# A transformer block on one core: gate, embedding projection and final norm laid out by tokens, the residual turned by VectorE and placed by SBUF-to-SBUF DMA

## The chip, the cores and the metric

One core of one Trainium2 chip runs the whole block in one program. The metric is the device time of an execution in microseconds; three executions of the kernel before were timed. The trace is of one further execution, with a span (first to last instruction) and a time of its own.

## The reference, cut to what matters

512 tokens, width 1024, float32. A mixer (mLSTM heads and sparse attention) and its output projection come first, then a convolutional feed-forward, then a gated per-layer embedding and a final norm:

```python
x = x + jnp.concatenate([m_out, a_out], axis=-1) @ w_out[i]
x = x + conv_ffn(rms_norm(x, ln2_g[i]), w_up[i], conv_w[i], conv_b[i], w_down[i])   # d_ff 2048
gate = jax.nn.sigmoid(rms_norm(x, ple_norm_g[i]) @ w_ple_gate[i])                   # 1024 x 1024
x = x + gate * (p[i] @ w_ple_proj[i])                                               # p: 512 x 256
return rms_norm(x, final_g)
```

with `rms_norm(x, g) = x * rsqrt(mean(x * x) + 1e-6) * g` over the 1024 features of a token.

## The kernel before, in words

Activations lie by features: the residual `X` is [128 features, 8 blocks, 512 tokens], so a sum over features runs over partitions and blocks, and a factor that belongs to a token is a row along the free dimension that has to be spread over all partitions. Every product in full precision is three matmuls in float32r: each operand is split into a high part (ScalarE copy, names ending in h) and a low part (VectorE subtraction, ending in l), and high times high, high times low and low times high are summed in PSUM. Weight blocks of 512 KB come in by SP's DMA queue into two raw buffers, are split into two pairs of buffers, and are used in the order of a list of jobs (`st`). A scheduler decides how the instructions of the code are interleaved on each engine; each engine then runs its list in order, and waits where an operand is not ready.

The last part of the program, which the change touches:

- **Down jobs** `wd{b}{half}` (b = 0 to 7): 48 matmuls of 512 columns into `pd{b}`; VectorE adds to `X[:, b]`, `sum_squares` makes the gate's operands `x3h`, `x3l` from it and adds squares to `acc3`.
- **Norm n3** (`start_norm`): four small matmuls sum `acc3` over partitions, VectorE does a reciprocal square root by Newton steps on [128 tokens, 4] (`n3yc`), four PE transposes and a ScalarE copy spread it as rows (`n3rb`).
- **Gate, output blocks 0 to 3** (`g0` to `g3`, `pg`): 24 matmuls of 512 columns each; the weight block is the stationary operand, the tokens move. `ple_evac` then multiplies by `n3rb` (VectorE), takes tanh (ScalarE), combines with the projected embedding `pp` and adds to `X` (VectorE), squares (ScalarE) and adds the squares into `acc4` (VectorE), and scales by the final gain (ScalarE).
- **Gate, blocks 4 to 7**: the weights `wgr` are split into `wres` and stay; two parts of 256 tokens, in each 4 x 24 matmuls of 256 columns, so that the first 256 tokens can be finished early.
- **End** (`start_finish`, `finish`): for the first part the sums, Newton steps, two PE transposes (`n40pb`) and products on GpSimd and VectorE run beside the second part's matmuls. For the second part a matmul with ones sums and spreads in one (`n4ps`), then follow a ScalarE reciprocal square root, three VectorE steps on 128x256, and products and output DMAs by feature blocks.

The embedding's projection `pp_job` runs much earlier, between the mLSTM heads, with 48 matmuls of 512 columns.

## Time and profile before

| | us |
|---|---|
| three timed executions | 646.04, 646.11, 647.53 (median 646.11) |
| the profiled execution's own time | 645.6 |
| its span | 643.8 |
| PE busy in the span | 623.0 (97%) |
| VectorE (DVE) busy | 429.9 (67%) |
| ScalarE (ACT) busy | 318.8 (50%) |
| GpSimd (POOL) busy | 42.7 (7%) |

The span leaves out 1.8 us of the profiled time. A busy share is a mean over stages that have different limits, so the stages at the end are read one by one.

### The profile page before, as it was taken

Reading aid. Unit: us, or ns where it says so; the run is one execution under the profiler, and the core shown is the slowest. Engines: PE = TensorE matmul, PEld = TensorE weight load, DVE = VectorE, ACT = ScalarE, POOL = GpSimd, SP = SyncE. Lnnn points to the kernel's source line nnn. Section 1 sums busy time; section 2 is a strip of 40 time slices with the busy share of each in tenths; the row PEclk is TensorE's granted clock in tenths of the full one; section 3 lists DMA queues with packets and bytes.
Section 4 is the critical chain, followed back from the end, with each engine's and each line's share of the span. In section 5 each row is a group of like instructions: output and inputs, shape, how many; then the busy total and the mean of one; then the engine's idle time right before and its main releaser. Section 6 shows DMA issues by size and latency. Waiting matters only on the chain.

```text
span 643.8 us, 8563 instructions
## 1 busy us (share of the span) xinstructions
PE 623.0 (97%) x3099; PEld 505.1 (78%) x3099; DVE 429.9 (67%) x868; ACT 318.8 (50%) x663; POOL 42.7 (7%) x92
## 2 busy tenths in 40 slices
PE   8997999999999999999999999999999999999993
PEld 6886877777777777787788888888888888888892
DVE  6898558888878977784876565655555334346766
ACT  7457445677656755654645333333343323233642
POOL 0400005211111200000000000000000000000003
PEclk9999999999999999999999999999999999999997
DMA  8712044311121153012233222222332323233203
GB/s 327 282 30 87 2 130 108 89 34 38 62 67 33 36 195 98 34 48 83 67 113 100 94 94 94 97 96 98 99 98 99 99 98 99 98 99 115 82 1 131
DMA packets 19673, 60.39 MB, mean 94 GB/s; under 512 B 2280, under 2 KB 4712, under 8 KB 19564
## 3 DMA queue, kind: packets, MB, share of 16 engines
q1 hardware_dynamic: 18096, 57.43, 26.9%
q0 software_dynamic: 1248, 2.16, 1.5%
q8 instruction: 24, 0.39, 0.2%
q10 hardware_dynamic: 288, 0.28, 0.2%
q14 instruction: 17, 0.14, 0.1%
HBM read 56.18 MB, written 2.10 MB: 91 GB/s over the span
## 4 chain that ended last, share of the span: by engine, by line
PE 82%; DVE 10%; ACT 4%; issue 1%; DMA 1%; DVEq 0%; ACTq 0%
PE pu L415 8%; PE pu L419 8%; PE pu L416 8%; PE pd L415 5%; PE pd L416 5%; PE pd L419 5%; PE pt L784 2%; PE pmq L416 2%; PE pmq L415 2%; PE pmq L419 2%; PE pv L792 2%; PE pmv L332 1%; PE pg L407 1%; PE ms L953 1%; PE pc L368 1%
## 5 line engine op out<-in xcount | busy, mean ns | idle before, releaser
L1075 ACT ACTIVATE u<-zv 128x512 fp32r<-128x512 f32 x16 | 10.1, 633 | 45.3 <-DVE zv L1073 45.3
L1072 DVE TENSOR_TENSOR zv<-pu,n2rb 128x512 f32<-128x512 f32 x16 | 11.1, 691 | 31.3 <-PE pu L419 31.3
L787 ACT ACTIVATE ph<-pt 128x512 fp32r<-128x512 f32 x40 | 23.5, 597 | 17.0 <-PE pt L784 16.4
L757 POOL TENSOR_SCALAR E<-E,rr 128x512 f32<-128x512 f32 (+3 forms) x32 | 21.2, 663 | 159.7 <-DVE rr L754 113.4
L788 DVE TENSOR_TENSOR pl<-pt,ph 128x512 fp32r<-128x512 f32 x40 | 27.0, 684 | 6.6 <-ACT ph L787 6.2
L1062 DVE TENSOR_TENSOR zg<-pu,n2rb 128x512 f32<-128x512 f32 x16 | 11.1, 692 | 26.0 <-PE pu L419 24.6
L784 PE MATMUL pt<-cols,E 128*128 128x128 f32 x160 | 27.8, 275 | 0.4 <-DVE E L759 0.3
L1088 DVE TENSOR_TENSOR X<-pd,X 128x512 f32<-128x512 f32 x8 | 5.5, 691 | 31.9 <-PE pd L419 31.9
L784 PEld LDWEIGHTS pt<-cols,E 128*128 128x128 f32 x160 | 20.0, 140 | 7.2 <-DVE E L759 2.6
L1065 ACT ACTIVATE cv<-zg,cols 128x512 f32<-128x512 f32 x16 | 13.1, 816 | 20.1 <-DVE zg L1062 20.1
L1068 ACT ACTIVATE cv<-cv 128x512 f32<-128x512 f32 x16 | 10.1, 631 | 24.6 <-DVE cv L1067 24.6
L751 ACT ACTIVATE E<-s,nm 128x384 f32<-128x384 f32 (+2 forms) x48 | 22.2, 471 | 0.0
L265 DVE TENSOR_TENSOR acc<-acc,sq 128x512 f32<-128x512 f32 (+1 forms) x30 | 19.1, 636 | 0.9 <-ACT sq L261 0.7
L792 PE MATMUL pv<-ph,V 128*128 128x512 f32 x40 | 18.7, 467 | 0.4 <-ACT ph L787 0.3
L261 ACT ACTIVATE sq<-X 128x512 f32<-128x512 f32 (+1 forms) x24 | 13.5, 560 | 11.0 <-DVE X L1129 11.0
L407 PE MATMUL pg<-x3h,wres 128*128 128x256 f32 x64 | 18.3, 285 | 0.0
L1076 DVE TENSOR_TENSOR u<-zv,u 128x512 fp32r<-128x512 f32 x16 | 11.1, 692 | 10.5 <-ACT u L1075 10.5
L408 PE MATMUL pg<-x3l,wres 128*128 128x256 f32 x64 | 18.1, 283 | 0.0
L409 PE MATMUL pg<-x3h,wres 128*128 128x256 f32 x64 | 18.1, 283 | 0.0
L1061 POOL MEMSET zg<- 128x2 f32 x16 | 1.5, 99 | 243.3 <-DVE cv L1067 150.7
L794 PE MATMUL pv<-pl,V 128*128 128x512 f32 x40 | 16.7, 418 | 0.0
L741 DVE TENSOR_REDUCE nm<-s 128x2 f32<-128x768 f32 (+2 forms) x24 | 16.4, 682 | 0.0
(1052 smaller groups left out, 2024.3 us busy)
## 6 DMA issues: line engine op xcount, KB each, us to landing
X<-in_xg SPq DMA_DIRECT2D x1, 2048.0 KB, 8.3
wgr<-in_w_pg SPq DMA_DIRECT2D x4, 512.0 KB, 3.6
s1r<-in_w_s SPq DMA_DIRECT2D x3, 672.0 KB, 9.0
xT<-in_xg SPq DMA_DIRECT2D x3, 514.0 KB, 8.3
rawx<-in_cmp_w SPq DMA_DIRECT2D x3, 512.0 KB, 6.3
Q<-hlq POOLq DMA_DIRECT2D x12, 128.0 KB, 3.4
out_y<-X SPq DMA_DIRECT2D x5, 256.0 KB, 2.2
rawx<-in_w_in SPq DMA_DIRECT2D x2, 512.0 KB, 11.1
```

The costliest lines, as they stand in the source:

```text
L265: return VE.tensor_add(acc[:, :n], acc[:, :n], sq[:, :n])
L407: TE.matmul(ps, wh[:, kw], rh[:, kx, n], start=first, stop=False)
L408: TE.matmul(ps, wh[:, kw], rl[:, kx, n], start=False, stop=False)
L415: TE.matmul(ps, wh[:, w], rh[:, x, n], start=first and j == 0, stop=False)
L416: TE.matmul(ps, wh[:, w], rl[:, x, n], start=False, stop=False)
L419: TE.matmul(ps, wl[:, w], rh[:, x, n], start=False, stop=last and j == len(kx) - 1)
L751: SE.activation(e, p, AF.Exp, bias=nm[:, b:b + 1], accum_out=rs[:, b:b + 1])
L757: GE.tensor_scalar(e, e, rr[:, b:b + 1], 0.0, op0=ALU.mult, op1=ALU.add)
L784: TE.transpose(pt[:, r * 128:(r + 1) * 128], Es[r][:, c0:c0 + 128], ident)
L787: SE.activation(ph, pt, AF.Copy)
L788: VE.tensor_sub(pl, pt, f32(ph))
L792: TE.matmul(pv, vs, ph, start=first, stop=False)
```

## The change

Gate, embedding and final norm are computed with tokens on the partitions. The gate's stationary operand is now a block of 128 tokens of `x3h` or `x3l`, and 512 columns of weights move past it (`psg[t]` for the first half of the output features, `pg1{t}` for the second). The n3 factor of a token is then one number per partition and goes in as the scale of the tanh (`sc`); the rows `n3rb` and their transposes go. The sum of squares of a token is a sum along the free dimension, taken by the squaring instruction's accumulator into `ss`; the n4 factor is one number per partition too. The last 128 tokens' second half is computed in two pieces of 256 columns (`CUT`), and only that last tile uses the ScalarE reciprocal square root; the others use Newton steps on [128, 1]. GpSimd has no part in it any more. The final gain comes as a full tile `gF`.

The residual has to be turned for this: after each down job VectorE transposes `X[:, b]` in squares of 32 (`turn`), and after blocks 3 and 7 sixteen DMAs each, from SP's queue, move 32 partitions' worth from `xturn` to their place in `xo` (`moves`; 64 KB each, in runs of 512 bytes). The features of a token come out permuted; the weights' columns are permuted on the way in and the output on the way out, outside the timed program. `pp_job` computes the projection by tokens, with the operands in exchanged roles.

The diff, cut to the new code; the bodies of the functions of the same names that stand above go out.

```diff
     def pp_job(c):
         def run(wh, wl):
+            for t in range(NT):
+                ts = slice(t * 128, (t + 1) * 128)
+                ps = pG(f"ppp{c}{t}")
+                for k in range(2):
+                    TE.matmul(ps, phl[:, 0, k, ts], wh[:, k], start=k == 0, stop=False)
+                    TE.matmul(ps, phl[:, 1, k, ts], wh[:, k], start=False, stop=False)
+                    yield 0.43
+                for k in range(2):
+                    TE.matmul(ps, phl[:, 0, k, ts], wl[:, k], start=False, stop=k == 1)
+                    yield 0.22
+                SE.activation(ppt[NT * c + t], ps, AF.Copy, scale=0.5)
+        st.add(f"pp{c}", a["w_pp"][:, c], [128, 2, 512], run)
...
     def start_norm(norm, acc, name):
         def stats():
             yc = rstd_stats(acc, name)
+            if norm is n3:
+                norm["yc"] = yc
+                return
...
+    xturn = [None]
+
+    def turn(b, dst):
+        VE.transpose(dst[:, :, :, b % 4].rearrange("p t c j -> p (t c) j"),
+                     X[:, b].rearrange("p (c j) -> p c j", j=32))
+        if b % 4 == 3:
+            for q in range(4):
+                st.after(T_TURN * (1 + q), lambda q=q: moves(b // 4, q, dst))
+
+    def moves(g, q, src):
+        for c in range(4):
+            nc.sync.dma_start(xo[32 * c:32 * c + 32, :, q // 2, q % 2 * 256 + g * 128:q % 2 * 256 + g * 128 + 128],
+                              src[32 * q:32 * q + 32, :, c].rearrange("p t b j -> p t (b j)"))
...
     def down_job(b, half):
...
+                if b % 4 == 0:
+                    xturn[0] = fpool.tile([128, NT, 4, 4, 32], F32, bufs=1, name=f"xturn{b}", tag="xturn")
+                st.after(T_TURN, lambda: turn(b, xturn[0]))
...
+    xo = fpool.tile([128, NT, 2, 512], F32, bufs=1, name="xo")
...
+    gF = main.tile([128, 2, 512], F32, tag="mixa", name="gF")
+    nc.sync.dma_start(gF, a["gF"])
+    ss = fpool.tile([128, NT, 3], F32, bufs=1, name="ss")
+    sc = fpool.tile([128, NT], F32, bufs=1, name="sc")
+
+    def scale_of():
+        yc = n3["yc"]
+        VE.tensor_scalar(sc, yc, 0.5, None, op0=ALU.mult)
 
+    def ple_evac(t, h, ps, c0, c1, part):
+        z = t2k("zz")[:, c0:c1]
+        last = SE.activation(z, ps[:, c0:c1], AF.Tanh, scale=sc[:, t:t + 1])
+        VE.scalar_tensor_tensor(z, z, 1.0, ppt[NT * h + t][:, c0:c1], op0=ALU.add, op1=ALU.mult)
+        o = xo[:, t, h, c0:c1]
+        VE.tensor_add(o, o, z)
+        sq = t2k("sq")
+        if t == NT - 1 and part == 2:
             pre = SE.activation(warm, epsc, AF.Abs_reciprocal_sqrt)
             behind(pre, last, "the table is loaded behind the last tanh")
+            VE.scalar_tensor_tensor(sq[:, c0:c1], o, 1.0, o, op0=ALU.mult, op1=ALU.mult,
+                                    accum_out=ss[:, t, part:part + 1])
         else:
+            SE.activation(sq[:, c0:c1], o, AF.Square, accum_out=ss[:, t, part:part + 1])
+
+    def finish(t):
+        orow = out[t * 128:(t + 1) * 128].rearrange("p (h n) -> p h n", h=2)
+        v = small.tile([128, 1], F32, tag="nrv", name=f"n4v{t}")
+        if t < NT - 1:
+            VE.tensor_add(v, ss[:, t, 0:1], ss[:, t, 1:2])
+            VE.tensor_scalar(v, v, 1.0 / D, EPS, op0=ALU.mult, op1=ALU.add)
+            y = newton_rsqrt(v, 1, f"n4{t}")
+            SE.activation(xo[:, t, 0], xo[:, t, 0], AF.Copy, scale=y)
+            VE.scalar_tensor_tensor(xo[:, t, 1], xo[:, t, 1], y, gF[:, 1], op0=ALU.mult, op1=ALU.mult)
+            nc.sync.dma_start(orow, xo[:, t])
+            return
+        VE.scalar_tensor_tensor(v, ss[:, t, 2:3], 1.0 / D, vlast, op0=ALU.mult, op1=ALU.add)
+        y = small.tile([128, 1], F32, tag="nry", name="n4y")
+        w = small.tile([128, 1], F32, tag="nrt", name="n4w")
+        u = small.tile([128, 1], F32, tag="nru", name="n4u")
+        SE.activation(y, v, AF.Abs_reciprocal_sqrt)
+        VE.tensor_scalar(u, v, -0.5, None, op0=ALU.mult)
+        VE.tensor_mul(xo[:, t, 1, CUT:], xo[:, t, 1, CUT:], gF[:, 1, CUT:])
+        VE.scalar_tensor_tensor(w, y, u, y, op0=ALU.mult, op1=ALU.mult)
+        VE.scalar_tensor_tensor(w, w, 1.5, y, op0=ALU.add, op1=ALU.mult)
+        SE.activation(xo[:, t, 0], xo[:, t, 0], AF.Copy, scale=w)
+        VE.tensor_scalar(xo[:, t, 1], xo[:, t, 1], w, None, op0=ALU.mult)
+        nc.sync.dma_start(orow[:, 1], xo[:, t, 1])
+        nc.scalar.dma_start(orow[:, 0], xo[:, t, 0])
...
+    CUT = 512 - LASTW
+    vlast = fpool.tile([128, 1], F32, bufs=1, name="vlast")
+    sa = pSa("pga")
+    psg = [sa[:, 0], sa[:, 1], pG("pg2"), pG("pg3")]
+
+    def gate_job(c):
         def run(wh, wl):
+            for t in range(NT):
+                ts = slice(t * 128, (t + 1) * 128)
+                for j in range(2):
+                    k = 2 * c + j
+                    TE.matmul(psg[t], x3h[:, k, ts], wh[:, j], start=k == 0, stop=False)
+                    TE.matmul(psg[t], x3l[:, k, ts], wh[:, j], start=False, stop=False)
+                    TE.matmul(psg[t], x3h[:, k, ts], wl[:, j], start=False, stop=k == KB - 1)
+                    yield 0.66
+                if c == 3 and t < 3:
+                    ple_evac(t, 0, psg[t], 0, 512, 0)
+            if c == 2:
+                scale_of()
+        st.add(f"g{c}", a["w_pg"][:, 0, 2 * c:2 * c + 2], [128, 2, 512], run)
+
+    for c in range(4):
+        gate_job(c)
+    wres = [main.tile([128, KB, 512], F32R, tag="B16", bufs=3, name=f"wres{i}") for i in range(2)]
+    for c in range(4):
+        st.until(f"g{c}")
+        raw = wpool.tile([128, 2, 512], F32, tag="raw", bufs=2, name=f"wgr{c}")
+        nc.sync.dma_start(raw, a["w_pg"][:, 1, 2 * c:2 * c + 2])
+        SE.activation(wres[0][:, 2 * c:2 * c + 2], raw, AF.Copy)
+        VE.tensor_sub(wres[1][:, 2 * c:2 * c + 2], raw, f32(wres[0][:, 2 * c:2 * c + 2]))
+
+    for t in range(NT):
+        ts = slice(t * 128, (t + 1) * 128)
+        ps = (pSb, pV, pT, pT)[t](f"pg1{t}")
+        cuts = ((0, 512),) if t < NT - 1 else ((0, CUT), (CUT, 512))
+        for part, (c0, c1) in enumerate(cuts):
+            if part:
+                ps = pG("pg1last")
             for k in range(KB):
+                TE.matmul(ps[:, c0:c1], x3h[:, k, ts], wres[0][:, k, c0:c1], start=k == 0, stop=False)
+                TE.matmul(ps[:, c0:c1], x3l[:, k, ts], wres[0][:, k, c0:c1], start=False, stop=False)
+                TE.matmul(ps[:, c0:c1], x3h[:, k, ts], wres[1][:, k, c0:c1], start=False, stop=k == KB - 1)
+                if part == 0 and k == 1 and t == 0:
+                    ple_evac(3, 0, psg[3], 0, 512, 0)
+                if part == 0 and k == 5:
+                    VE.tensor_mul(xo[:, t, 0], xo[:, t, 0], gF[:, 0])
+            ple_evac(t, 1, ps, c0, c1, 1 + part)
+            if t == NT - 1 and part == 0:
+                VE.tensor_mul(xo[:, t, 1, 0:c1], xo[:, t, 1, 0:c1], gF[:, 1, 0:c1])
+                VE.tensor_add(vlast, ss[:, t, 0:1], ss[:, t, 1:2])
+                VE.tensor_scalar(vlast, vlast, 1.0 / D, EPS, op0=ALU.mult, op1=ALU.add)
+        finish(t)
...
+    def turned(w):
+        return w.reshape(-1, 8, 4, 32).transpose(0, 2, 1, 3).reshape(-1, D)
```

Three places in the engines' lists show what moved. The first is SP's list of DMA issues around the last down jobs and the gate; `wd..r`, `g.r` and `wgr` are loads of weight blocks into the raw buffers. Before:

```order
L146 DMA wd51r<-in_w_down 128x1024
L146 DMA wd60r<-in_w_down 128x1024
L146 DMA wd61r<-in_w_down 128x1024
...
L146 DMA g2r<-in_w_pg 128x1024
L1160 DMA wgr_5312<-in_w_pg 128x1024
L146 DMA g3r<-in_w_pg 128x1024
L1160 DMA wgr_5356<-in_w_pg 128x1024
L1160 DMA wgr_5394<-in_w_pg 128x1024
L1177 DMA out_y<-X 128x256 x4
```

and with the change (`xo<-xturn` are the moves, x16 stands for sixteen in a row):

```order
L142 DMA wd51r<-in_w_down 128x1024
L1094 DMA xo<-xturn_4728 32x4x128 x16
L142 DMA wd60r<-in_w_down 128x1024
...
L1138 DMA gF<-in_gF 128x1024
L142 DMA g2r<-in_w_pg 128x1024
L1094 DMA xo<-xturn_5009 32x4x128 x8
L1213 DMA wgr_5327<-in_w_pg 128x1024
L142 DMA g3r<-in_w_pg 128x1024
L1094 DMA xo<-xturn_5009 32x4x128 x8
L1213 DMA wgr_5370<-in_w_pg 128x1024
L1213 DMA wgr_5416<-in_w_pg 128x1024
```

Sixteen moves now stand ahead of the load `wd60r`, eight ahead of the second `wgr` and eight ahead of the third; the gain `gF` is one more load.

The second is ScalarE's list from the first gate tiles on. Before (`zz` is the tanh, `sq` the squares, `X<-X,cols` the gain, `wres` the split of resident weights):

```order
L1137 ACTIVATE X<-X,cols 128x512
L1125 ACTIVATE zz<-zz 128x512
L1161 ACTIVATE wres_5195<-wgr_5394 128x1024
L261 ACTIVATE sq<-X 128x512
L1137 ACTIVATE X<-X,cols 128x512
L1125 ACTIVATE zz<-zz 128x512
L261 ACTIVATE sq<-X 128x512
L1125 ACTIVATE zz<-zz 128x256
L1137 ACTIVATE X<-X,cols 128x512
L261 ACTIVATE sq<-X 128x256
L1137 ACTIVATE X<-X,cols 128x256
L1125 ACTIVATE zz<-zz 128x256
```

With the change (`sq,ss` are squares with their sum in `ss`, `pga` holds tiles 0 and 1 of the first half, the last `pg` rows here tile 0 of the second half):

```order
L1148 ACTIVATE zz<-pga,sc 128x512
L1159 ACTIVATE sq,ss<-xo 128x512
L1148 ACTIVATE zz<-pga,sc 128x512
L1214 ACTIVATE wres_5224<-wgr_5370 128x1024
L1159 ACTIVATE sq,ss<-xo 128x512
L1148 ACTIVATE zz<-pg_5222,sc 128x512
L1214 ACTIVATE wres_5224<-wgr_5416 128x1024
L1159 ACTIVATE sq,ss<-xo 128x512
L1148 ACTIVATE zz<-pg_5223,sc 128x512
L1159 ACTIVATE sq,ss<-xo 128x512
L1148 ACTIVATE zz<-pg_5420,sc 128x512
L1159 ACTIVATE sq,ss<-xo 128x512
```

The gain has left this list, and each tanh but the first now stands directly behind the square of the tile before it.

The third is VectorE's list in the same stretch. Before, four operations a tile (row factor, combine, add, sum of squares):

```order
L1129 TENSOR_TENSOR X<-X,zz 128x512
L1162 TENSOR_TENSOR wres_5195<-wgr_5394,wres_5195 128x1024
L1124 TENSOR_TENSOR zz<-pg_5360,n3rb 128x512
L265 TENSOR_TENSOR acc_5193<-acc_5193,sq 128x512
L1128 SCALAR_TENSOR_TENSOR zz<-zz,pp 128x512
L1129 TENSOR_TENSOR X<-X,zz 128x512
L1124 TENSOR_TENSOR zz<-pg_5398,n3rb 128x256
L265 TENSOR_TENSOR acc_5193<-acc_5193,sq 128x512
L1128 SCALAR_TENSOR_TENSOR zz<-zz,ppPH_2657 128x256
L1129 TENSOR_TENSOR X<-X,zz 128x256
L1124 TENSOR_TENSOR zz<-pg_5432,n3rb 128x256
L265 TENSOR_TENSOR acc_5193<-acc_5193,sq 128x256
```

With the change, from the first tile of the gate on:

```order
L1149 SCALAR_TENSOR_TENSOR zz<-zz,pp 128x512
L1151 TENSOR_TENSOR xo<-xo,zz 128x512
L1231 TENSOR_TENSOR xo<-xo,gF 128x512
L1149 SCALAR_TENSOR_TENSOR zz<-zz,pp 128x512
L1151 TENSOR_TENSOR xo<-xo,zz 128x512
L1215 TENSOR_TENSOR wres_5225<-wgr_5370,wres_5224 128x1024
L1231 TENSOR_TENSOR xo<-xo,gF 128x512
L1149 SCALAR_TENSOR_TENSOR zz<-zz,pp 128x512
L1215 TENSOR_TENSOR wres_5225<-wgr_5416,wres_5224 128x1024
L1151 TENSOR_TENSOR xo<-xo,zz 128x512
L1231 TENSOR_TENSOR xo<-xo,gF 128x512
L1149 SCALAR_TENSOR_TENSOR zz<-zz,pp 128x512
```

The row factor and the sum of squares have left the list; the product with `gF` has come in, directly behind each add, and the splits of the last two `wgr` stand between the tiles.

## Rows read from the trace of the kernel before

**Rows 1.** The page's table of busy time: engine, busy us, share of the span, instructions.

```profile
PE 623.0 (97%) x3099; PEld 505.1 (78%) x3099; DVE 429.9 (67%) x868; ACT 318.8 (50%) x663; POOL 42.7 (7%) x92
```

**Rows 2.** Busy time by stage: the last down jobs, the gate's first half, its second half, and what follows the last gate matmul. Columns: from:to, length, then busy us (instructions) of PE, PEld, DVE, ACT, POOL, then granted clock, DMA share, GB/s.

```profile
563.00:584.70 21.70, 21.70 (x96) 17.83 (x95) 8.59 (x10) 6.49 (x9) 0.00 (x0) 1.00 0.32 97
584.70:607.90 23.20, 23.20 (x110) 19.34 (x109) 18.48 (x32) 13.76 (x19) 0.00 (x0) 1.00 0.36 114
607.90:631.50 23.60, 23.60 (x199) 23.58 (x197) 16.58 (x44) 10.53 (x23) 2.53 (x4) 1.00 0.02 7
631.50:643.80 12.30, 1.56 (x6) 0.59 (x4) 7.60 (x14) 3.10 (x6) 3.45 (x3) 0.72 0.46 160
```

**Rows 3.** PE in order of time: start, duration, line, operation. The first matmul of `wd60`, the first of the gate, the sums of n3, its transposes and the matmul behind them, the first of g3, the first of 256 columns, the first of the last 21 and the last.

```profile
562.76 0.40 PE L415 MATMUL pd<-u,wd60h 128*128 128x512 f32 x1
...
584.71 0.39 PE L407 MATMUL pg<-x3h,g0h 128*128 128x512 f32 x1
...
588.79 0.95 PE L292 MATMUL n3ps<-ones,acc 128*128 128x1 f32 x8
...
593.32 0.60 PE L311 MATMUL n3pb<-cols,n3yc 128*128 128x128 f32 x4
593.67 0.48 PE L415 MATMUL pg<-x3h,g1h 128*128 128x512 f32 x1
...
602.42 0.39 PE L415 MATMUL pg<-x3h,g3h 128*128 128x512 f32 x1
...
607.86 0.28 PE L407 MATMUL pg<-x3h,wres 128*128 128x256 f32 x1
...
629.01 0.28 PE L407 MATMUL pg<-x3h,wres 128*128 128x256 f32 x1
...
631.41 0.28 PE L409 MATMUL pg<-x3h,wres 128*128 128x256 f32 x1
```

**Rows 4.** DVE, ACT and SP in order of time behind the last gate matmul, in brackets the idle time before and what ended it.

```profile
631.73 0.42 DVE L1124 TENSOR_TENSOR zz<-pg,n3rb 128x256 f32<-128x256 f32 x1
632.65 0.40 ACT L1125 ACTIVATE zz<-zz 128x256 f32<-128x256 f32 x1
633.07 1.28 ACT L1131 ACT_TABLE_LOAD   x1
...
637.57 2.42 DVE L1174 TENSOR_TENSOR X<-X,n4y 128x512 f32<-128x512 f32 x3
...
639.91 0.47 DVE L1171 SCALAR_TENSOR_TENSOR X<-X,cols,n4y 128x256 f32<-128x256 f32 x1
640.05 0.91 SPq L1177 DMA_DIRECT2D out_y<-X  x2
```

**Rows 5.** Prices on ACT and DVE, grouped by line and form: busy us, mean ns of one, idle before. ACT tanh, square, copy with a scale by column, the accumulator's read; DVE combine, a factor by column, a step on two columns, the split of resident weights on both.

```profile
L1125 ACT ACTIVATE zz<-zz 128x512 f32<-128x512 f32 x4 | 2.5, 624 | 2.9 <-DVE zz L1124 2.9
L261 ACT ACTIVATE sq<-X 128x512 f32<-128x512 f32 x6 | 3.7, 624 | 3.3 <-DVE X L1129 3.3
L1137 ACT ACTIVATE X<-X,cols 128x512 f32<-128x512 f32 x4 | 2.9, 716 | 0.1
L967 ACT ACTIVATION_READ_ACCUMULATOR sqn<-mo 128x1 f32 x16 | 3.3, 205 | 0.0
L1128 DVE SCALAR_TENSOR_TENSOR zz<-zz,pp 128x512 f32<-128x512 f32 x4 | 2.8, 690 | 1.2 <-ACT zz L1125 1.1
L759 DVE TENSOR_SCALAR E<-E,rr 128x512 f32<-128x512 f32 x8 | 4.2, 523 | 0.0
L283 DVE TENSOR_TENSOR n40t<-n40t,n40y 128x2 f32<-128x2 f32 x1 | 0.2, 161 | 0.0
L1162 DVE TENSOR_TENSOR wres<-wgr,wres 128x1024 fp32r<-128x1024 f32 x4 | 4.9, 1222 | 0.8 <-ACT wres L1161 0.8
L1161 ACT ACTIVATE wres<-wgr 128x1024 fp32r<-128x1024 f32 x4 | 4.2, 1052 | 0.8 <-DMA wgr<-in_w_pg 0.7
```

**Rows 6.** DVE and ACT in order of time around the adds of down blocks 3 and 4 and the split of `wd60`.

```profile
543.42 0.68 DVE L265 TENSOR_TENSOR acc<-acc,sq 128x512 f32<-128x512 f32 x1
546.77 1.23 DVE L153 TENSOR_TENSOR wd50l<-wd50r,wd50h 128x1024 fp32r<-128x1024 f32 x1 [2.67 <-ACT wd50h L152]
...
556.65 1.06 ACT L152 ACTIVATE wd60h<-wd60r 128x1024 fp32r<-128x1024 f32 x1 [2.69 <-issue]
```

**Rows 7.** SP's DMA issues in order of time: start, us on the queue, tile.

```profile
223.67 0.66 SPq L853 DMA_DIRECT2D X<-in_xg  x1
...
548.03 0.33 SPq L146 DMA_DIRECT2D wd60r<-in_w_down  x1
...
589.21 0.33 SPq L1160 DMA_DIRECT2D wgr<-in_w_pg  x1
```

**Rows 8.** DMA queues (packets, MB, share of 16 engines over the span) and issues by line (KB each, median us from issue to landing).

```profile
q10 hardware_dynamic: 288, 0.28, 0.2%
...
wgr<-in_w_pg SPq DMA_DIRECT2D x4, 512.0 KB, 3.6
...
Q<-hlq POOLq DMA_DIRECT2D x12, 128.0 KB, 3.4
out_y<-X SPq DMA_DIRECT2D x5, 256.0 KB, 2.2
...
out_y<-X SPq DMA_DIRECT2D x5, 128.0 KB, 1.7
```

115 lines of the change are left out of this document (10 added, 105 removed).

## The prediction

> **What bounds the kernel now.** I read the table of busy time first: PE works 97% of the span [rows 1]. A mean hides stages, so the table by stage came next [rows 2]. In the last down jobs and in both halves of the gate PE is busy in every microsecond (21.70 of 21.70, 23.20 of 23.20, 23.60 of 23.60), at granted clock 1.00, and VectorE and ScalarE have room: up to 631.5 us the time is what PE issues. The last 12.3 us are different: PE works 1.56 of them, VectorE 7.60. There the order of time shows a chain, from the row factor at 631.73 through tanh and table load to the last product, which ends at 640.38 (639.91 + 0.47), its DMA, and the span's end at 643.80 [rows 4]. So two things can pay: fewer PE microseconds before 631.5, and a shorter chain behind it.
>
> **PE.** A matmul of 512 columns takes 0.227 us from issue to issue (18 of them from 584.71 to 588.79), one of 256 columns 0.120 us (20 from 629.01 to 631.41) [rows 3]. The gate's first half keeps its 96 matmuls of 512 columns. In its second half 192 of 256 (23.04 us) become 72 of 512 and 48 of 256 (16.32 + 5.76 = 22.08): 0.96 saved. The n3 transposes cost 0.35 from 593.32 to 593.67 and 0.1 in the slower matmul behind them: 0.45 saved. The n4 sums and transposes of the first part cost what is left between the start of the 192 and their end: 607.86 + 23.04 is 630.90, the last one's slot ends at 631.53, so 0.63 saved. Together 2.0: the last gate matmul's slot ends near 629.5, and its result is there at 629.6.
>
> **The evacuation, tile by tile.** Before, VectorE takes four operations a tile and never makes PE wait. Now the lists tie ScalarE and VectorE together: a square waits for the combine and the add of its tile, and the next tile's tanh stands behind that square. One tile thus costs a whole round. Prices from [rows 5]: the tanh is between the one with a fixed scale (0.624) and a copy with a scale by column (0.716), and since the scale is by column now I take 0.72; combine 0.69; add 0.69, as it is the same product form; the square 0.624 and the accumulator's read 0.205, which starts some 0.07 before the square ends, so 0.76; and 0.03 for each handover. A round is 2.9.
>
> The first tile's last matmul is the ninth of g3 in PE's new list. g3 began at 602.42 [rows 3], now 0.45 sooner, so its first tile is ready at about 604.1. Tanhs then start at 604.1, 607.0 and 609.9. Between tiles 2 and 3 ScalarE has to split the last `wgr` (1.05) and VectorE its low part (1.22) and that of the one before, so the next start is 614.1; then 617.0 (first tile of the second half, which PE has ready by 614.5) and 619.9. From there VectorE carries the Newton steps too, some eleven operations of 0.16 a tile [rows 5] (0.20 where each waits for the one before), and the final product of the tile with factor and gain, about 0.75. That makes the rounds 4.1, 3.9 and, for the half tile, 3.6: starts at 624.0, 627.9 and, for the last 256 columns, 631.5. PE has these ready at 629.6. So the evacuation is the new bound, and ends about 1.9 later than PE alone would allow. PE itself waits for nothing: the splits come at or just ahead of their use, and PE's list goes on with tile 1 where tile 0 lacks them.
>
> **The end.** From 631.5: tanh of 256 columns 0.45 (0.40 in [rows 4], with a scale by column a little more), combine and add 0.45 each, then the square with its sum on VectorE. No row shows a sum beside a product there; it is at least the product (0.42) and at most that and a read like ScalarE's (0.2): I take 0.62. That is 633.6. A step on one column 0.16, the square root on ScalarE 0.2 (its table, 1.28, loads from 631.9 and is there), two steps of 0.2, 634.5. The last scaling runs on both engines, 0.523 and 0.716 for 512 columns [rows 5], to 635.25. From the last product to the span's end it is 3.42 now [rows 4]; two DMAs of 256 KB close the program instead of one of 128 KB, 2.2 against 1.7 to land [rows 8], so I add 0.5: 639.2. The chain behind the last tanh is 7.7 where it was 12.1 from the row factor on: no matmul in between, one column instead of 256 in the Newton steps, and none of the four products at the end that took 2.8 from 637.57 on.
>
> **The sum.** Span 643.8 less 639.2: 2.0 from PE, 4.4 from the end, 1.9 given back to the evacuation, 4.6 gained (rounded). The profiled execution took 645.6, so 641.0; it lies 0.5 under the median of the three runs, so against that median 641.5.
>
> **Turning and moving.** Eight VectorE transposes of 128x512 have no row. Bounds: the 0.523 of the fastest 512-column form above, and four times a product, 2.8. Either way VectorE idles 2.67 before it splits `wd50` [rows 6], so I take 0.7 and it costs nothing; behind block 7 it moves the split of g2 by as much, with 4 us to spare.
>
> The moves are what can hurt, for SP issues in order. The first sixteen stand ahead of the load of `wd60`. They can start when block 3 is turned, about 544.8 (the sum of squares ends at 544.1 [rows 6]). That load went out at 548.03 [rows 7], but `wd60` was split only at 556.65, when its buffer came free [rows 6], and PE wants it at 562.76 [rows 3]. With 3.6 to land [rows 8] and 1.06 to split it may go out as late as 558.2. So the sixteen have 13.4 us, 0.84 each; below that they are hidden. Two blocks take 21.95 from 562.76 to 584.71 [rows 3], so block 7 is turned 43.9 after block 3, at 588.7. Of the second group eight stand ahead of the second `wgr` (issued at 589.21 [rows 7]) and eight ahead of the third. That `wgr` has to land (3.7 with its issue), its two parts are split (1.05, 1.22), and g3's low part (1.22) is split behind it on VectorE; PE uses that part at 603.1, five matmuls into g3. That leaves 7.2 us for eight, 0.90 each. What does one cost? On the queue 0.33 as a load, up to 0.66 as the one with eight times as many runs [rows 7]. On the engines: 288 packets of about 1 KB took 0.2% of 16 engines' span [rows 8], 71 ns each, so eight packets per engine 0.57. In flight up to eight share the landing of 1.7 (output) to 3.4 (the only SBUF-to-SBUF row, from POOL's queue [rows 8]): 0.2 to 0.43. I take 0.45, near the issue, and the range is 0.33 to 0.66: hidden. The table of queues thus speaks for cheap small packets. The Trainium skill (DMA: Bandwidth & Descriptors, Bandwidth) says to batch DMAs to 1 MiB and gives 0.95 us for one of 64 KB; by that, as an estimate, the sixteen take 15.2, PE waits 1.8 there and 0.4 in the second group, and the sum would be 643.7 (rival C); no row here shows a transfer of 64 KB.
>
> **The rivals.** A, the evacuation keeps up with PE: the tanh at its lower price and more overlap between neighbours on an engine. Then the last tanh starts at 629.6 and the time is 639.6. For it: by the walk above it is 2.5 behind PE at the second half's first tile and only 0.2 at the third. Against it: the last two starts are 2.9 of PE apart, and the rounds there are 3.6 to 3.9. B, the rounds are dearer: a sum on VectorE or a handover that costs more, or no overlap between neighbours on an engine (0.08 each over some 30 operations): 2.3 more, 643.8. D, on the other side, with C as its mild form: the moves hold SP's queue, each for longer than 0.84. Where the first group makes PE wait 16 times the excess over 0.84 and the second 8 times that over 0.90, the gain is gone at 1.05 each (3.4 + 1.2); at 1.2 PE waits 5.8 and 2.4 and the time is 649.7; at 1.7, each waiting for its landing, it is beyond 660. C is the middle between 0.84 and 1.05, 0.95: PE waits 1.8 and 0.4, 643.7. For C and D: eight in flight at most, and no row of a hardware-queue move from SBUF to SBUF. Against it: the last two output DMAs, of 1 KB runs, left the queue in 0.91 together [rows 4].
>
> **Numbers.** Chances: the forecast (640.3 to 643.0) 0.56, A 0.16, B 0.13, C 0.05, D 0.10. This kernel's measurement tells 0.3%, 1.9 us, from no change: faster is below 644.2. The forecast, A and about half of B and C are faster: 0.81; the rest of B and C is the same, with the mildest of D: 0.09; slower 0.10. The range takes in A, B and C: 639.0 to 645.2.
>
> **What would show it.** Right: sixteen moves in under 10 us and no gap in PE at 563; last gate matmul near 629.5; the last tanh 1 to 3 us behind it, with ScalarE's squares waiting for VectorE's adds; 3.5 to 4 from the last tanh to the last scaling; SP's last DMA near 635. Wrong: PE waiting for `wd60` or for `wres`, a VectorE transpose that waits for the moves of the group before, or a last tanh that starts with PE's end or 4 us behind it.

## The result and the profile after

The changed kernel takes 641.18 us (median of 4: 639.04, 640.82, 641.54, 642.14) where the kernel before takes 646.21 (646.04 to 647.53): a ratio of 0.9913, 95% interval 0.9895 to 0.9931, 5.0 us. The forecast was 641.5. The profiled execution took 639.04, with a span of 637.2; it is the shortest of the four, for a reason that the experiments make likely.

The page's table of busy time, against [rows 1]:

```profile
PE 618.9 (97%) x3013; PEld 498.4 (78%) x3013; DVE 426.6 (67%) x882; ACT 314.1 (49%) x656; POOL 36.6 (6%) x85
```

Busy time by stage, columns as in [rows 2]: the last down jobs, the gate's first half, its second half, what follows.

```profile
561.80:583.80 22.00, 22.00 (x98) 18.02 (x97) 9.87 (x12) 6.74 (x9) 0.00 (x0) 1.00 0.36 115
583.80:606.80 23.00, 23.00 (x106) 18.76 (x105) 12.21 (x25) 7.51 (x12) 0.00 (x0) 1.00 0.65 183
606.80:628.90 22.10, 22.10 (x121) 19.21 (x119) 18.72 (x57) 11.53 (x25) 0.00 (x0) 1.00 0.12 47
628.90:637.20 8.30, 0.12 (x2) 0.00 (x0) 4.10 (x16) 3.51 (x7) 0.00 (x0) 0.81 0.34 131
```

PE is still busy in every microsecond up to the last gate matmul. The second half is 1.5 shorter, and what follows it 8.3 instead of 12.3. PE in order of time, the rows that answer to [rows 3] (first matmul of `wd60`, of the gate, of its second half, the last):

```profile
561.79 0.40 PE L411 MATMUL pd<-u,wd60h 128*128 128x512 f32 x1
...
583.79 0.39 PE L1197 MATMUL pga<-g0h,x3h 128*128 128x512 f32 x1
...
606.79 0.39 PE L1225 MATMUL pg<-wres,x3h 128*128 128x512 f32 x1
...
628.74 0.28 PE L1227 MATMUL pg1last<-wres,x3h 128*128 128x256 f32 x1
```

The gate starts 0.92 sooner than before, though nothing in front of it was made shorter; an experiment below tells why. So the change is read from the first gate matmul on: from there to the span's end it is 53.41 where it was 59.09, 5.68 less.

One stage in front of the gate even became longer. The 96 matmuls of the output projection's second half, from the first of `wom0` to the first of `wu00`, before and then after:

```profile
298.82 0.40 PE L407 MATMUL pom<-mixm,wom0h 128*128 128x512 f32 x1
...
320.81 0.40 PE L407 MATMUL pu<-x2h,wu00h 128*128 128x512 f32 x1
```

```profile
297.10 0.40 PE L403 MATMUL pom<-mixm,wom0h 128*128 128x512 f32 x1
...
319.51 0.40 PE L403 MATMUL pu<-x2h,wu00h 128*128 128x512 f32 x1
```

They take 22.40 instead of 21.99, and the down jobs from `wd00` to the gate 0.2 more as well. Both numbers are the same in the run without turning and moving (below), so these are not the cause; what is stays open.

The turning and moving, VectorE, SP and ScalarE in order of time (against [rows 6, 7]):

```profile
543.00 0.70 DVE L1086 STREAM_TRANSPOSE xturn<-X 128x512 f32<-128x512 f32 x1
543.79 10.35 SPq L1094 DMA_DIRECT2D xo<-xturn  x16
554.24 0.53 SPq L142 DMA_DIRECT2D wd60r<-in_w_down  x1
555.87 0.71 DVE L1086 STREAM_TRANSPOSE xturn<-X 128x512 f32<-128x512 f32 x1 [1.79 <-DMA xo<-xturn]
557.88 1.06 ACT L148 ACTIVATE wd60h<-wd60r 128x1024 fp32r<-128x1024 f32 x1 [4.92 <-DMA wd60r<-in_w_down]
```

Sixteen moves hold SP's queue for 10.35, 0.65 each. `wd60` goes out 6.2 later than in [rows 7], and ScalarE now waits for its landing; it is split by 558.94, 2.85 before PE takes it. The turn of block 4 waits 1.79 for the moves to leave `xturn`, on an engine with room.

The evacuation, ScalarE's tanhs from the first tile on, then the closing of the third tile (scaled with `n42y`), the last tanh and the last scaling (against [rows 4]):

```profile
603.41 0.69 ACT L1148 ACTIVATE zz<-pga,sc 128x512 f32<-128x512 f32 x1 [3.24 <-PE pga L1199]
606.22 0.67 ACT L1148 ACTIVATE zz<-pga,sc 128x512 f32<-128x512 f32 x1
...
616.17 0.67 ACT L1148 ACTIVATE zz<-pg,sc 128x512 f32<-128x512 f32 x1
619.02 0.67 ACT L1148 ACTIVATE zz<-pg,sc 128x512 f32<-128x512 f32 x1
623.31 0.69 ACT L1148 ACTIVATE zz<-pg,sc 128x512 f32<-128x512 f32 x1 [0.31 <-PE pg L1227]
...
629.48 0.72 ACT L1168 ACTIVATE xo<-xo,n42y 128x512 f32<-128x512 f32 x1 [0.56 <-DVE n42y L280]
630.11 0.46 ACT L1148 ACTIVATE zz<-pg1last,sc 128x256 f32<-128x256 f32 x1
...
633.10 0.72 ACT L1181 ACTIVATE xo<-xo,n4w 128x512 f32<-128x512 f32 x1 [0.66 <-DVE n4w L1180]
```

The rounds take 2.8 to 2.9, as reckoned. But at 623.31 ScalarE waits for PE again: it has caught up. The last tanh is then late for another reason than the rounds: the scaling of the third tile stands ahead of it in ScalarE's list and waits for that tile's last Newton step.

### The profile page after: what moved, and what is told of

It reads as the page before. It is cut to its first block, busy times and chain, and to the rows that moved or that the text cites. A ratio compares the mean times of both kernels' runs of the same rounds, so it can differ in the third digit from the quotient of the medians.

```text
span 637.2 us, 8437 instructions
## 1 busy us (share of the span) xinstructions
PE 618.9 (97%) x3013; PEld 498.4 (78%) x3013; DVE 426.6 (67%) x882; ACT 314.1 (49%) x656; POOL 36.6 (6%) x85
## 5 line engine op out<-in xcount | busy, mean ns | idle before, releaser
L261 DVE TENSOR_TENSOR acc<-acc,sq 128x512 f32<-128x512 f32 x21 | 14.4, 684 | 0.1
L964 PEld LDWEIGHTS mo<-vo,mw 128*128 128x128 f32 x80 | 11.4, 191 | 2.1 <-issue 0.7
L755 DVE TENSOR_SCALAR E<-E,rr 128x512 f32<-128x512 f32 (+3 forms) x32 | 13.0, 405 | 0.1
L749 DVE RECIPROCAL rr<-rs 128x3 f32<-128x3 f32 x32 | 5.5, 171 | 11.1 <-ACT E L747 11.1
L747 ACT ACTIVATE Ec<-s,nm 128x32 f32<-128x32 f32 x24 | 6.9, 286 | 11.8 <-DVE nm L737 11.6
```

What stands on the lines that cost most here:

```text
L261: return VE.tensor_add(acc[:, :n], acc[:, :n], sq[:, :n])
L747: SE.activation(e, p, AF.Exp, bias=nm[:, b:b + 1], accum_out=rs[:, b:b + 1])
L755: VE.tensor_scalar(e, e, rr[:, b:b + 1], None, op0=ALU.mult)
L964: TE.matmul(po[:, 0:130], Ws[j][:, (i - j) * 128:(i - j + 1) * 128], vones(j, h), start=(j == 0), stop=(j == i))
```

## The experiments

"The stretch" is always from the first gate matmul to the end of the span, 53.41 in the changed kernel and 59.09 in the one before. Times given as "behind the gate's start" count from the same matmul. The runs with the moves doubled and halved, with the squares late and with 256 columns have one execution each, the profiled one.

**Are the moves hidden by SP's slack? Each issued twice.**

```diff
+            nc.sync.dma_start(out.rearrange("(t p) n -> p t n", p=128)
+                              [32 * c:32 * c + 32, :, q * 256 + g * 128:q * 256 + g * 128 + 128],
+                              src[32 * q:32 * q + 32, :, c].rearrange("p t b j -> p t (b j)"))
```

> The changed kernel with every move issued twice; the second copy goes from the turned tile to a part of the output that the real output overwrites later. Theory (the moves are hidden only because sixteen of them stay within the 13.4 us that SP has ahead of the load of wd60): at 0.65 each, as in the changed kernel, thirty-two take 20.7, wd60 goes out near 565 instead of 554.2, is there and split near 569.5, and PE, which wanted it at 561.8, waits 7 to 8 us in one piece; in the second group sixteen ahead of the second wgr take 10.4 where 7.2 are free, 3 more. Sum 8 to 11 us over the changed kernel, 649 to 652. Rival (PE does not hang on SP's queue, the weights are far enough ahead): no piece of PE idle over 0.5 us before the gate, time within 1.5 us of the changed kernel.

Measured 660.13. PE's first matmul of `wd60`, SP's load of it, and stretches of PE around it (columns as above, the granted clock third from the end):

```profile
565.73 0.39 SPq L142 DMA_DIRECT2D wd60r<-in_w_down  x1
570.58 0.80 PE L411 MATMUL pd<-u,wd60h 128*128 128x512 f32 x1 [7.47 <-ACT wd60h L148]
```

```profile
572.00:574.00 2.00, 2.00 (x6) 1.59 (x5) 1.01 (x1) 0.00 (x0) 0.00 (x0) 0.50 0.57 168
576.00:578.00 2.00, 2.00 (x10) 1.67 (x9) 0.00 (x0) 0.21 (x1) 0.00 (x0) 1.00 0.25 102
```

The first wait is 7.47, as the theory says, and the rival is out. The sum is not: the span is 21.1 longer, not 8 to 11. Behind the idle time PE runs at half clock (0.50, the 1.2 GHz level) until past 574, and `wd60` to `wd70` takes 13.36 where it took 11.00. From the gate's start on it is 9.9 more; 4.4 of that is a further wait, for `wres`, priced at 3, with the clock at half behind it again. (1.2 was there before the moves began, from a low clock near 64 that comes up below.) This PE wait cost more than its length.

**What sets a move's time on SP? Each cut in two.**

```diff
-            nc.sync.dma_start(xo[32 * c:32 * c + 32, :, ...], src[32 * q:32 * q + 32, :, c]...)
+            for t in (slice(0, 2), slice(2, 4)):
+                nc.sync.dma_start(xo[32 * c:32 * c + 32, t, ...], src[32 * q:32 * q + 32, t, c]...)
```

> The changed kernel with every move cut in two: sixty-four moves of 32 KB, 64 runs of 512 bytes each, instead of thirty-two of 64 KB with 128 runs. Theory (SP's time for a move goes by its runs): 0.30 to 0.40 each, thirty-two in 10 to 12 us, wd60 goes out by 556 and PE does not wait for it; time within 1.5 us of the changed kernel. Rival (SP's time goes by the number of DMAs, whatever is in them): 0.6 to 0.65 each, 20 us, PE waits 7 us or more for wd60 and again in the gate, as in the run with every move issued twice, 650 or more.

Measured 658.63. SP and PE in order of time:

```profile
546.12 20.82 SPq L1095 DMA_DIRECT2D xo<-xturn  x32
567.04 0.52 SPq L142 DMA_DIRECT2D wd60r<-in_w_down  x1
572.03 0.79 PE L411 MATMUL pd<-u,wd60h 128*128 128x512 f32 x1 [7.74 <-ACT wd60h L148]
```

Again 0.65 each, with half the bytes and half the runs. SP's time goes by the number of moves; the rival holds for moves of this kind. It does not say that every DMA costs the same: a load takes 0.33 [rows 7]. Cut into twice as many moves, the change would have lost all that it gains.

**What do turning and moving cost when hidden? Left out.** 

```diff
-                st.after(T_TURN, lambda: turn(b, xturn[0]))
...
+    GE.memset(xo, 0.0)
```

> The changed kernel without the eight transposes and the thirty-two moves; the residual is left out of the sum (its tile is filled with zeros by GpSimd). Theory (turning and moving is fully hidden): PE's first gate matmul and its last one stay where they are relative to each other (45.1 us from start to start, within 0.2), and the stretch from the first gate matmul to the end of the span stays at 53.4, within 0.3. Rival (32 small moves slow the weight loads or PE's neighbours by contention): the stretch, or the one from the down jobs to the gate, is shorter by 1 us or more and the time falls below 640.

Measured 643.5 (ratio to before 0.9956, 0.9942 to 0.9969): not shorter but longer. Up to the gate's fourth job nothing moves: `wd60` to the first gate matmul is 22.00 in both kernels, from there to `g3` 17.35 against 17.38. So the turning is hidden up to there. Behind it the scheduler had written another order, with the splits of the last two `wgr` ahead of the first tanh. ScalarE and PE in order of time:

```profile
604.11 1.06 ACT L1212 ACTIVATE wres<-wgr 128x1024 fp32r<-128x1024 f32 x1 [2.93 <-DMA wgr<-in_w_pg]
605.08 0.67 ACT L1146 ACTIVATE zz<-pga,sc 128x512 f32<-128x512 f32 x1
605.80 0.50 PE L1195 MATMUL pga<-g3h,x3h 128*128 128x512 f32 x1 [1.05 <-ACT zz L1146]
```

PE waits 1.05 for that tanh, since tiles 0 and 1 share the `pga` tile. The stretch, 56.23, thus says nothing on the moves.

**Is the evacuation the bound to the end? Squares behind the next tile's tanh.**

```diff
+        if owed:
+            behind(owed.pop()(), last, "the square stands behind the next tile's tanh")
...
+            sqr = lambda: SE.activation(sq[:, c0:c1], o, AF.Square, accum_out=ss[:, t, part:part + 1])
+            if h == 0 and t < 3:
+                owed.append(sqr)
```

> The changed kernel, but for the first three tiles of the gate's first half ScalarE squares a tile only behind the next tile's tanh, so that its list no longer waits through a whole round. Theory as the trace of the changed kernel has it (the rounds of 2.87 us hold the evacuation 3.8 us behind PE at the first tile of the second half, but PE takes 5.44 for a tile there and is the bound again at the third): the tanh of the first tile of the second half, 32.4 us after the first gate matmul in the changed kernel, comes 1.5 to 2.5 earlier, while the third tile's stays at 39.5 and the last tanh at 46.3, both within 0.3, and the stretch from the first gate matmul to the end of the span at 53.4, within 0.4. Rival as the prediction had it (the rounds are the bound to the end): the last tanh comes with PE's end, 45.2 to 45.4, and the stretch is 0.9 to 1.1 shorter.

Measured 639.44. The tanhs of the second half, in order of time:

```profile
613.87 0.69 ACT L1150 ACTIVATE zz<-pg,sc 128x512 f32<-128x512 f32 x1
617.90 0.69 ACT L1150 ACTIVATE zz<-pg,sc 128x512 f32<-128x512 f32 x1 [0.94 <-PE pg L1235]
623.81 0.67 ACT L1150 ACTIVATE zz<-pg,sc 128x512 f32<-128x512 f32 x1
630.29 0.45 ACT L1150 ACTIVATE zz<-pg1last,sc 128x256 f32<-128x256 f32 x1
```

Behind the gate's start (583.57) these are 30.30, 34.33, 40.24 and 46.72. The first comes 2.1 sooner, the last 0.4 later; the stretch is 53.83. Shorter rounds in the first half buy nothing at the end, so these rounds are not its bound. The third tile missed its 39.5: with more room the scheduler put the second tile's scaling in front of it.

**Does PE's end carry through? The second half in 256 columns, twice.** Both kernels cut the matmuls of the first three tiles in two; only the second has the lines with `behind`, which hold ScalarE's list and the place of VectorE's last combine behind the third tile's closing product as they are in the changed kernel.

```diff
+            for kk in range(KB * (c1 - c0) // 256):
+                k, m0 = kk % KB, c0 + kk // KB * 256
+                mm = slice(m0, m0 + 256)
+                TE.matmul(ps[:, mm], x3h[:, k, ts], wres[0][:, k, mm], start=k == 0, stop=False)
...
+            behind(last, closed[2][0], "as in the changed kernel")
+            behind(comb, closed[2][1], "as in the changed kernel")
```

> The changed kernel, but the first three token tiles of the gate's second half are computed in two runs of 256 columns instead of one of 512, with one evacuation a tile as before. PE: 72 matmuls of 512 columns become 144 of 256, at 0.227 and 0.120 us, so 0.94 us more. Theory as the prediction had it (the evacuation by tiles is the bound to the end): the last tanh, 1.1 us behind PE in the changed kernel, stays where it is relative to the first gate matmul (46.3 us after it, within 0.3), and the stretch from the first gate matmul to the end of the span stays at 53.4. Rival (at the third tile of the second half ScalarE waits for PE again, as the trace of the changed kernel has it with 0.31 us, so PE sets the end through that tile): the last tanh and the end come 0.6 to 0.95 later.

> Again the first three token tiles of the gate's second half in runs of 256 columns, but now with ScalarE's list held as it is in the changed kernel (the last tanh behind the third tile's scaling, as there) and VectorE's last tile behind the third tile's closing product. PE ends 0.9 later. Theory (PE sets the end through the third tile, whose tanh waits for PE): the last tanh 47.0 to 47.3 us after the first gate matmul instead of 46.3, and the stretch to the end of the span 54.1 to 54.4 instead of 53.4. Rival (the rounds of the evacuation set the end): the last tanh at 46.3 and the stretch at 53.4, both within 0.3.

Measured 641.47 and 641.44. PE's last matmul stands 45.87 and 45.88 behind the gate's start (44.95 before the edit), as reckoned. The last tanh of the first, then of the second kernel:

```profile
631.37 0.45 ACT L1148 ACTIVATE zz<-pg1last,sc 128x256 f32<-128x256 f32 x1
```

```profile
632.56 0.45 ACT L1148 ACTIVATE zz<-pg1last,sc 128x256 f32<-128x256 f32 x1
```

In the first it stands at 46.30, where it was, and alone would have spoken for the evacuation; but there the scheduler had put it ahead of the third tile's scaling, and the stretch grew to 54.63 all the same, as VectorE's closing product delayed the last combine. In the second it stands at 47.65, and the stretch is 54.79: 1.3 and 1.4 more for 0.93 of PE, 0.4 above the theory's sizes. The third tile in the second kernel, ScalarE's tanh and then VectorE:

```profile
625.35 0.69 ACT L1148 ACTIVATE zz<-pg,sc 128x512 f32<-128x512 f32 x1 [0.98 <-PE pg L1237]
```

```profile
626.40 0.75 DVE L1177 SCALAR_TENSOR_TENSOR xo<-xo,n41y,gF 128x512 f32<-128x512 f32 x1
627.07 0.69 DVE L1149 SCALAR_TENSOR_TENSOR zz<-zz,ppPL 128x512 f32<-128x512 f32 x1
```

and its combine in the changed kernel, where the second tile's closing product comes later, at 625.94:

```profile
624.03 0.69 DVE L1149 SCALAR_TENSOR_TENSOR zz<-zz,ppPL 128x512 f32<-128x512 f32 x1
```

The third tile's tanh waits 0.98 for PE and stands at 40.45 behind the gate's start, 0.93 later than in the changed kernel: PE and not the rounds sets that tile, and there the rival is out. Behind it the order was not held: VectorE has the second tile's closing product ahead of the third tile's combine, which begins 1.72 behind its tanh instead of 0.72. So it is not shown how much of the 1.3 at the last tanh is PE's and how much this order's.

**What delays the last tanh? The third tile's closing on GpSimd.**

```diff
+            if t == 2:
+                GE.tensor_mul(xo[:, t, 1], xo[:, t, 1], gF[:, 1])
+                GE.tensor_scalar(xo[:, t, 1], xo[:, t, 1], y, None, op0=ALU.mult)
+                GE.tensor_scalar(xo[:, t, 0], xo[:, t, 0], y, None, op0=ALU.mult)
```

> The changed kernel with the closing products of the third token tile (gain, then the factor on both halves) on GpSimd instead of ScalarE and VectorE. Theory (the last tanh is late only because ScalarE's scaling copy of the third tile, which waits for that tile's Newton steps, stands ahead of it in its list): the last tanh starts where PE has its tile ready, 45.2 to 45.4 us after the first gate matmul instead of 46.3, and the end comes 0.9 to 1.1 earlier, a stretch of 52.3 to 52.6. Rival (the lag is made by the rounds of tanh, combine, add and square before it): the last tanh moves by less than 0.3. A third way: GpSimd's products of 128x512 (1.5 us each as a product, 0.94 as a scaling) slow VectorE beside them or end after the last output of the other engines, and the end moves later.

Measured 642.84 (ratio to before 0.9953, 0.9935 to 0.9971), the stretch 55.52, 2.1 longer. The last tanh stands at 46.11, only 0.2 sooner, so this run settles nothing about what delays it. GpSimd and VectorE in order of time, two pairs that ran side by side:

```profile
628.71 1.50 POOL L1169 TENSOR_TENSOR xo<-xo,gF 128x512 f32<-128x512 f32 x1 [154.02 <-ACT sq L1159]
628.97 1.25 DVE L1165 TENSOR_TENSOR n4v<-ss 128x1 f32<-128x1 f32 x1
...
633.08 1.85 POOL L1170 TENSOR_SCALAR xo<-xo,n42y 128x512 f32<-128x512 f32 x1 [2.87 <-DVE vlast L1240]
633.53 0.80 DVE L1151 TENSOR_TENSOR xo<-xo,zz 128x256 f32<-128x256 f32 x1
```

The third way: a sum of one column, 0.15 alone, takes 1.25 and ends with GpSimd's product; an add of 0.42 takes 0.80, and GpSimd's scaling takes twice the 0.94 that eight of that size take earlier in the program. The Trainium skill (SBUF — State Buffer, SBUF: two separate sides) says that VectorE and GpSimd share a port pair which one of them holds for its whole instruction; by that one of two such instructions waits for the other's end. The first pair agrees: the sum ends with the product, at 630.22. The second agrees less well, for GpSimd's scaling began first and yet VectorE's add ended 0.6 before it.

**The same question by order alone.** The third tile's scalings go behind the last tile's square root (ScalarE) and Newton steps (VectorE).

```diff
+                    behind(i, after_se, "behind the last tile")
+                    behind(j, after_ve, "behind the last tile")
```

> The changed kernel with the closing of the third token tile put behind the last tile in both lists, without GpSimd: ScalarE scales its first half behind the square root of the last tile, VectorE multiplies its second half with the gain earlier and scales it behind the Newton steps of the last tile. Theory (the last tanh waits only for that closing): it starts 45.2 to 45.4 us after the first gate matmul instead of 46.3, and since the closing now costs 0.5 to 0.7 in front of the last scaling, the stretch from the first gate matmul to the end of the span is 52.4 to 52.9 instead of 53.4. Rival (what is moved back comes out on the path at full price, 0.49 on VectorE and 0.72 on ScalarE, and the larger last burst of output lands later): the tanh moves, the stretch stays at 53.2 or more. A second rival (rounds): the tanh does not move.

Measured 640.95 (ratio to before 0.9917, 0.9896 to 0.9939). The last tanh, then the DMA share and rate (last two columns) at the end:

```profile
629.47 0.47 ACT L1148 ACTIVATE zz<-pg1last,sc 128x256 f32<-128x256 f32 x1 [0.24 <-PE pg1last L1242]
```

```profile
634.00:635.00 1.00, 0.00 (x0) 0.00 (x0) 0.00 (x0) 0.00 (x0) 0.00 (x0) 0.80 0.98 389
635.00:636.00 1.00, 0.00 (x0) 0.00 (x0) 0.00 (x0) 0.00 (x0) 0.00 (x0) 0.50 0.99 377
```

The last tanh waits for PE now, 45.22 behind the gate's start, 1.1 sooner: that closing was what delayed it. Yet the stretch is 53.85. The last scaling ends 0.76 sooner, but 1 MB of output instead of 512 KB goes out in one burst, and the DMA engines are full (0.98, 0.99) for two microseconds. The first rival holds.

**Why do executions of one kernel differ by 3 us?** In the profile after, PE idles from 59.6 to 62.3, as before. ScalarE and PE there, and the stretches behind in the kernel before and in the one after:

```profile
60.71 0.63 ACT L646 ACTIVATE gt<-gt 4x512 f32<-4x512 f32 x1 [2.26 <-DVE gt L645]
61.24 1.04 ACT L148 ACTIVATE mv0h<-rawx 128x1024 fp32r<-128x1024 f32 x1
62.34 0.50 PE L328 MATMUL pmv<-mv0h,x1h 128*128 128x512 f32 x1 [2.76 <-ACT mv0h L148]
```

```profile
64.00:66.00 2.00, 2.00 (x7) 1.52 (x6) 1.94 (x3) 1.96 (x3) 0.00 (x0) 0.50 0.03 8
```

```profile
64.00:66.00 2.00, 2.00 (x10) 1.65 (x10) 1.94 (x3) 1.97 (x3) 0.00 (x0) 1.00 0.03 8
```

Same work, half the clock in the first (0.50), full in the second. It puts the first 1.66 behind at `mv1` (71.82 against 70.16); 0.92 of that is left at the gate, since the changed kernel loses about 0.7 on the way (the longer output projection and down jobs above). So 0.92 of the 6.6 between the two profiled executions is not the change. The clock fell there in seven of ten profiled executions with that idle time. The edit emits the exponential later and puts it behind the split:

```diff
+        late = SE.activation(gt_, gt_, AF.Exp, scale=-1.0)
+        behind(late, splits["mv0"], "the split of mv0 goes first")
```

> The changed kernel with one thing moved far from the change: in the mLSTM gates ScalarE's exponential, which waits 2.3 us for VectorE's scan, goes behind the split of mv0 instead of ahead of it, so that PE no longer stands idle from 59.2 to 62.4. The granted clock fell to half in or right behind that idle time in the profiled execution of the kernel before and of four variants of the changed one, not in that of the changed kernel itself. Theory (the idle time brings the low clock, and it is why executions of one kernel differ): the clock stays at 1.00 from 58 to 70, PE starts mv0 near 59.5, the first gate matmul comes at 581.2 to 582.0 instead of 583.8, the median falls by 3 to 4.5 to 636.7 to 638.2, and the executions lie within 1.5 us of each other instead of 3.1. Rival (the low clock comes with something else that happens then, or the work behind mv0 is bound by VectorE, which is busy 4.8 of 5 us there): the clock falls as before and the median falls by less than 2.5.

> The kernel before, with ScalarE's exponential behind the split of mv0 and nothing else. Both kernels share that stage, so this pair (638.2 for the changed kernel with the same edit) is the change without the chance of the low clock. Theory (the low clock and the idle time have nothing to do with the change; the change is worth what the two traces show from the first gate matmul to the end of the span, 59.09 less 53.41): executions within 1.5 us, no low clock from 58 to 70, median 643.4 to 644.2, 5.2 to 6.0 above the changed kernel. Rival (the medians of the unchanged pair, 5.0 apart, are the change's true worth, since something ahead of the gate in the changed kernel gives back 0.7): 642.7 to 643.3.

The changed kernel with it takes 638.22 (638.12 to 638.28; ratio to before 0.9871, 0.9856 to 0.9887), the kernel before with it 643.74 (643.09 to 644.79; 0.9969, 0.9956 to 0.9982). The profiles have no low clock from 58 to 70 in either; the spread falls from 3.1 to 0.2 in the changed kernel. The gate starts at 583.11, later than reckoned, since a wait of 1.36 for the split of mv1 opens up. So the idle time brings the low clock, though not in every execution. It is not the whole spread: in the kernel before 1.7 stays, more than the 1.5 expected, with a mean granted clock of 0.995 in the shortest execution and 0.992 in the longest, and no trace shows where the clock falls in those.

Between the two medians stand 5.5, between the two profiled spans 5.3 (641.8 and 636.5), and 5.9 if each is taken from the kernel before in its own round. The stretch alone is again 5.7 shorter, but the changed kernel's gate starts 0.44 later (583.11 against 582.67). So the theory holds for the size, and what the rival names, something given back ahead of the gate, is there too: the change is worth 5.3 to 5.9, nearly all of the 5.68.

**Both, and a better version.** The first kernel joins the two orders and gives the gate's second transposes a bank of their own; the second has the bank, the mLSTM order and two more of the same kind, and the original closing.

```diff
-            pt = pV(f"pgt{src}")
+            pt = (pV if src == 0 else pT)(f"pgt{src}")
...
+        behind(scan, splits["cw01"][1], "the low part of cw01 goes first")
...
+            behind(late, splits["mv1"][0], "the split of mv1 goes first")
```

> The order of the closing (as in the kernel with the third tile's closing behind the last tile) and the mLSTM order (as in the kernel with mv0 split ahead of the exponential) together, and the second pair of gate transposes in a bank of its own, so that PE does not wait 1.5 us for VectorE near 47. Theory (the three lie one behind another in time and add): 0.5 to 1.0 from the closing, 3 to 4.5 from mv0, 0 to 1.5 from the bank (VectorE is close to the bound there): 634.5 to 637.5, faster than both kernels. Rival (VectorE is the bound from 45 to 63, so the bank gives nothing and mv0's low half comes late): 637.5 to 639.5.

> The changed kernel with its original closing and four places of order in the mLSTM stage: the second pair of gate transposes in a bank of its own, VectorE's second scan behind the low part of cw01, ScalarE's exponential behind the split of mv0, and ScalarE's tanh of the compression behind the split of mv1. Theory (PE's waits of 1.5 us near 48, 3.1 near 60 and 1.4 near 69 go, none longer than 0.8 is left between 44 and 75, and the clock stays up): 635.0 to 637.0, 1.2 to 3 under the version with mv0's order alone (638.2), executions within 1 us. Rival (VectorE, busy 4.8 of 5 us from 45 to 65, is the bound, so what one wait loses another gains, and a longer one brings the low clock back, as with the bank alone): 637.5 to 639.5.

The first measured 638.74 (ratio 0.9879, 0.986 to 0.9897): the closing gave nothing (above), and with the bank alone the idle times gathered into one of 1.73 before 59.32, with the clock at 0.50 behind it; its rival holds, though that wait is for the low part of cw01 and not of mv0. The second took 636.11 (635.85 to 637.61; ratio to before 0.9858, 0.9836 to 0.988), 10 us faster than the kernel before and 5 than the changed one; one of the five executions lies 1.5 above the others. Its longest wait of PE in that stage is 0.5 (columns: us in total, times, longest):

```profile
PE pc L493 <- DVE cw01l L150: 0.5, 1, 0.5
```

## Why the prediction was right

Point by point, times behind the gate's start.

- **PE.** From the first gate matmul to the end of the last slot 45.07 instead of 46.82: 1.75, where the prediction had 2.0. The second half came out (22.07 against the reckoned 22.08). Of the 0.25 missing, 0.1 is the sums of n3 (0.89 instead of 0.81) and 0.1 a matmul into `pga` that goes behind the first tanh.
- **Rounds.** Tanh starts were walked as 19.4, 22.3, 25.2, 29.4, 32.3 and 35.2; they are 19.6, 22.4, 25.3, 29.5, 32.4 and 35.2. This part stands.
- **"The evacuation is the new bound, and ends about 1.9 later."** This step failed. It is 1.1 late, and not through the rounds: the evacuation has caught up at the third tile (39.5, waiting for PE), shorter rounds in the first half change nothing, and with a later PE that tile comes later by as much. What is late is one scaling that stands ahead of the last tanh in a list; once that scaling goes behind, the last tanh starts with PE's end (45.22). The walk had the third tile 0.2 off PE, but added rounds of 3.9 and 3.6 behind it without asking what stands in ScalarE's list there.
- **The end.** Last tanh to the end of the last scaling 3.71, reckoned 3.75. From there to the span's end 3.38, reckoned 3.92: the added 0.5 for the larger output did not come. That term was over-sized.
- **Moves.** Hidden, with 2.85 to spare. Their price was mis-sized: 0.65 at the range's upper end, not 0.45. The sentence that worked it out from packets and landings looked at the wrong place; for these moves SP's own time decides, half as large or not. The Trainium skill (DMA: Bandwidth & Descriptors, Bandwidth) gives 0.95 us for 64 KB, as time on the DMA engines of a load from HBM that GpSimd issues, and advises to batch DMAs. No run here measures that figure, and 0.65 is the time on SP's queue; but the advice fits, since twice as many moves of half the size held the queue twice as long (20.82). The turn of block 4 did wait for the moves, which the prediction had listed as a sign against it; on VectorE that cost nothing.
- **Rival D** was priced too low (649.7 at 1.2 each; 652.1 at 1.3 by the same sum). The doubled moves, at 1.3 for each original one, took 660: the half clock behind PE's wait and the later `wres` were not in the sum.
- **The sum.** The stretch was reckoned as 54.49 and is 53.41: 0.25 worse on PE, 0.8 better on the lag, 0.5 on the landing. So the end gained 5.68 where 4.6 was forecast. Ahead of the gate the prediction had put no change at all, and there the changed kernel gives back 0.7 in both pairs of profiles (from `mv1` to the gate 513.63 against 512.89, and 513.73 against 513.06 with the exponential moved). That leaves 5.0, and 641.2 against 641.5. That the numbers meet so closely is luck in good part: 1.1 more gained in the stretch than forecast, and against it a loss of 0.7 that was not reckoned at all.

## What to carry to other kernels

Count small moves by their number on the issuing queue, and set that against how early the next load must go out; bytes and landing times come second. When an evacuation follows PE, walk it tile by tile up to the last one: a bound that has caught up once is no longer the bound, and what then decides is the list order of one or two instructions. And before believing an experiment on one piece, see what else the scheduler moved: in four of these twelve the scheduler had also written another order than the one under test, once although half of the order was held.

## What was unexpected of the hardware

- A PE wait of 2.8 us came with half clock, in or right behind it, in seven of ten profiled executions and with full clock in three, with the same instructions. One of 1.73 was followed by half clock too, in the one execution seen; one of 1.36 (behind the mv0 edit, near 69) was not, in two, nor one of 1.5 near 49, in twelve. With the longest wait gone, the spread over executions fell from 3.1 to 0.2 us in the changed kernel, but only to 1.7 in the one before.
- Matmuls of 512 columns that the change did not touch go 0.233 us apart in the output projection's second half, where they went 0.229 apart before; why is open.
- SP takes 0.65 us from one move between places of SBUF to the next, for 128 runs of 512 bytes as for 64, twice the 0.33 of a load of 512 KB.
- A VectorE instruction on one column took 1.25 us beside a GpSimd product of 128x512.
- VectorE turns 128x512 in squares of 32 in 0.70 us, the price of a product.
